# Merging two branches by pairs of column chunks, with the gates' tanh issued earlier and attention scores kept negated

## The chip, the cores and the metric

The kernel runs on one core of a Trainium2 chip. The metric is the device time of one execution in microseconds (us). Five engines work side by side, each through its own instructions in order: PE multiplies matrices, DVE does elementwise work and reductions, ACT does elementwise functions (exponential, logarithm, tanh) and casts, POOL does small extra work, SP issues transfers. An engine that must wait for another holds everything that is queued behind the waiting instruction.

## The reference

One layer of a decoder trunk over 512 tokens of 1024 channels, cut to what bears on the change:

```
h    = rmsnorm(x)
proj = h @ w_in                      # mLSTM q,k,v,o,i,f | attention q,k,v | gates ga, gb
hm   = head_rmsnorm(mlstm(...))      # 4 heads of 128, branch A
# branch B: differential attention, 4 heads, query blocks of 128
s    = q k^T / 8 + bias              # two score matrices per head, causal
a    = softmax(s1) - lam * softmax(s2)
hd   = head_rmsnorm(a @ v) * (1 - lam_init)
ya, yb = (sigmoid(o) * hm) @ w_br_m, hd @ w_br_d
x    = x + (sigmoid(ga) * ya + sigmoid(gb) * yb) @ w_out
# then the gated feed-forward layer, a per-layer embedding and a last norm
```

## The kernel before

Everything is kept channel-major: 128 channels in the partitions, the 512 tokens along the row. Every float32 product is made of three products of rounded parts (`mm3`, L94 to L98: high by high, low by high, high by low), so a product over k blocks of 128 is 3k matmuls of 128x512. Each weight chunk (128x1024) goes through `wload` (L100 to L107): SP loads `raw`, ACT casts it to `whi` (L88), DVE makes the rest `wlo` (L89). Each of the three has two buffers, so a cast waits until PE has read the chunk that is two before it.

The order of the work up to the merge is the string ORDER (projections, mLSTM heads m0 to m3, attention heads a0 to a3, their norms A and N, and eight gate projections ga0 to ga3 and gb0 to gb3). A scheduler then interleaves the instructions of each engine by priority and dependence; within an engine the order is fixed once it is built.

An attention head (`attention`, L459) takes four query blocks, each with two score matrices. For a score matrix PE makes `ds` (L468), DVE adds the bias and takes the row's greatest value (L472), negates it (L475), ACT takes the exponential with that as bias and sums the row (L476), DVE takes the reciprocal of the sum (L477). Then DVE scales and combines the two (L480, L481), PE turns the result (`at`, L487), ACT and DVE split it (`aph`, `apl`, L88 and L89), PE multiplies it with v (`av`). `attention_end` (L491) squares `av`, PE sums the squares over the channels (`hd3ss` for head 3, L168 and L169), and `rsqrt_of` (L152) makes the inverse root: Ln (L157) and Exp (L159) on ACT, Square (L160), two DVE steps (L161, L162). A product (L497) and a split give `hdh` and `hdl` (L91, L92), which PE multiplies with the branch weights.

The merge loop (L550 to L565) makes one column chunk of 128 channels at a time: both gates' tanh (L555), eight weight blocks that hold the chunk's four blocks for `ya` and its four for `yb`, 24 matmuls into two result banks of the group `mm` (four banks), then DVE and ACT combine them into `mxh`, `mxl`. Gates of the chunks 4 to 7 are projected just before their chunk, 24 matmuls each. Tanh and Ln need different function tables on ACT; a load of a table is an instruction of its own, and the gates' tanh are held by `issue_after(last_exp.ins)` behind the last Exp of a norm.

Of the kernel before, what the change touches and what calls it, by code (L numbers as in the profile page):

```python
# [11 lines left out]
F32 = mybir.dt.float32  # L12
F32R = mybir.dt.float32r
AF = mybir.ActivationFunctionType
ALU = mybir.AluOpType

P = 128
S = 512
D = 1024
KD = D // P  # L20
# [35 lines left out]
def trunk_kernel(ctx, tc, xT, pT, par, biasT, lamv, w_if, w_in, w_v, w_br, w_out, w_up,  # L56
                 w_down, w_gate, w_ple, gfin, out):
    nc = tc.nc
# [3 lines left out]
    tp = ctx.enter_context(tc.tile_pool(name="tp", bufs=1))  # L62
# [6 lines left out]
    def rt(tag, name):  # L69
        return big.tile([P, S], F32R, tag=tag, name=name, bufs=NBUF[tag])  # L70
# [5 lines left out]
    def ps(tag, name, n=S):  # L76
        return pp.tile([P, S], F32, tag=tag, name=name, bufs={"mm": 4, "sc": 2, "acc": 2}[tag])[:, :n]
# [8 lines left out]
    def split(hi, lo, src, scale=None):  # L86
        if scale is None:
            nc.scalar.copy(hi, src)  # L88
            nc.vector.tensor_sub(lo, src, f(hi))  # L89
        else:  # L90
            nc.scalar.activation(hi, src, AF.Copy, scale=scale)  # L91
            nc.vector.scalar_tensor_tensor(lo, src, scale, f(hi), op0=ALU.mult, op1=ALU.subtract)  # L92
# [7 lines left out]
    def wload(src, n=1024):  # L100
        raw = wp.tile([P, 1024], F32, tag="raw", name="raw", bufs=2)
        hi = wp.tile([P, 1024], F32R, tag="whi", name="whi", bufs=2)
        lo = wp.tile([P, 1024], F32R, tag="wlo", name="wlo", bufs=2)
        with tc.high_priority(offset=180):
            nc.sync.dma_start(raw[:, :n], src)
            split(hi[:, :n], lo[:, :n], raw[:, :n])
        return hi, lo  # L107
# [4 lines left out]
    def proj(o, w, k0, acts, start=True, stop=True):  # L112
        n = len(acts)
        for i, a in enumerate(acts):
            mm3(o, wk(w, k0 + i), a, start and i == 0, stop and i == n - 1)
# [14 lines left out]
    lnb = cp.tile([P, 1], F32, name="lnb")  # L130
# [16 lines left out]
            nc.scalar.activation(q, src, AF.Square)  # L147
            nc.vector.tensor_add(acc, acc, q)

    last_exp = None  # L150

    def rsqrt_of(r, v, a, before=None):  # L152

        if before is not None:
            with tc.issue_after(before.ins):
                nc.scalar.preload_act_table_set("natural_log_exp_and_others")
        nc.scalar.activation(r, v, AF.Ln, scale=2.0 ** -LN_SHIFT)  # L157
        nonlocal last_exp
        last_exp = nc.scalar.activation(r, r, AF.Exp, scale=-0.5, bias=lnb)  # L159
        nc.scalar.activation(a, r, AF.Square)  # L160
        nc.vector.scalar_tensor_tensor(a, v, -0.5, a, op0=ALU.mult, op1=ALU.mult)  # L161
        nc.vector.scalar_tensor_tensor(r, a, 1.5, r, op0=ALU.add, op1=ALU.mult)  # L162
# [19 lines left out]
    acc = tt("mo", "acc")  # L182
# [273 lines left out]
        return hi, lo  # L456


    def attention(hh, q, k):  # L459
        av = []  # L460
        for i in range(NB):
            n = (i + 1) * P
            nw = max(n, 2 * P)
            es, sums = [], []
            for z in range(2):
                s = ps("sc", f"ds{hh}{i}{z}", nw)
                for b in range(2):
                    nc.tensor.matmul(s, lhsT=q[z][:, i * P:(i + 1) * P], rhs=k[z][b][:, :nw],  # L468
                                     start=b == 0, stop=b == 1)
                e = tt("e" if z == 0 else "rb", f"e{z}", n)  # L470
                mx = tp.tile([P, 4], F32, tag="mx", name="mx", bufs=8)
                nc.vector.tensor_tensor_reduce(  # L472
                    out=e, in0=s[:, :n], in1=bias[hh][:, S - n:], scale=1.0, scalar=-3.0e38,
                    op0=ALU.add, op1=ALU.max, accum_out=mx[:, 0:1])
                nc.vector.tensor_scalar_mul(mx[:, 1:2], mx[:, 0:1], -1.0)  # L475
                nc.scalar.activation(e, e, AF.Exp, bias=mx[:, 1:2], accum_out=mx[:, 2:3])  # L476
                nc.vector.reciprocal(mx[:, 3:4], mx[:, 2:3])  # L477
                es.append(e)
                sums.append(mx[:, 3:4])
            nc.vector.tensor_scalar(es[1], es[1], sums[1], nlam, op0=ALU.mult, op1=ALU.mult)  # L480
            nc.vector.scalar_tensor_tensor(es[0], es[0], sums[0], es[1], op0=ALU.mult, op1=ALU.add)  # L481
            av.append(es[0])
        o = ps("acc", f"av{hh}")
        for j in range(NB):
            tps = ps("sc", f"at{hh}{j}", S - j * P)
            for i in range(j, NB):
                nc.tensor.transpose(tps[:, (i - j) * P:(i - j + 1) * P], av[i][:, j * P:(j + 1) * P], ident)  # L487
            weighted("a", j, lambda a, b: split(a, b, tps), dv, hh, (o,))
        return o
# [12 lines left out]
    def gate(c, name):  # L502
        o = ps("mm", name)
        proj(o, win(c), 0, h)
        t = tt("x", name)
        nc.vector.tensor_mul(t, o, rB)
        return t
# [3 lines left out]
    mq, mk, dq, dk, mo, sums, hm, hd, ga, gb = ({} for _ in range(10))  # L511
    for step in ORDER.split():
        what, i = step[:-1], int(step[-1])
# [18 lines left out]
        elif what == "bias":  # L532
            bias, nlam = make_bias(), make_nlam()
# [12 lines left out]
    hm, hd = ([t[i] for i in range(H)] for t in (hm, hd))  # L546


    mixed = []
    for j in range(KD):  # L550
        ta = ga[j] if j in ga else gate(20 + j, "ga")
        tb = gb[j] if j in gb else gate(28 + j, "gb")
        with tc.issue_after(last_exp.ins):
            for t in (ta, tb):
                nc.scalar.activation(t, t, AF.Tanh, scale=0.5)  # L555
        w = wload(w_br[j])
        oa, ob = ps("mm", "ya"), ps("mm", "yb")
        proj(oa, w, 0, hm)
        proj(ob, w, 4, hd)
        nc.vector.scalar_tensor_tensor(ta, ta, 1.0, oa, op0=ALU.add, op1=ALU.mult)  # L560
        nc.vector.scalar_tensor_tensor(tb, tb, 1.0, ob, op0=ALU.add, op1=ALU.mult)
        nc.vector.tensor_add(ta, ta, tb)
        hi, lo = rt("v", f"mxh{j}"), rt("v", f"mxl{j}")
        split(hi, lo, ta, 0.5)
        mixed.append((hi, lo))  # L565


    x2, h2 = [], []
    acc = tt("mo", "acc")
# [27 lines left out]
    for c in range(KF):  # L597
# [4 lines left out]
        hi, lo = rt(gtag[c], f"gh{c}"), rt(gtag[c], f"gl{c}")  # L602
# [175 lines left out]
def _chunks(w):  # L778

    k, n = w.shape  # L780
    return w.reshape(k // P, P, n // P, P).transpose(2, 1, 0, 3).reshape(n // P, P, k)
# [25 lines left out]
def _pack(x, p, rel_bias, norm_mix_g, w_in, b_if, m_conv_w, m_conv_b, m_norm_g, da_lambda, da_norm_g,  # L807
          w_br_m, w_br_d, w_out, norm_ffn_g, w_up, ffn_conv_w, ffn_conv_b, w_down, norm_ple_g,
          w_ple_gate, w_ple, norm_final_g):
    w = w_in[0]  # L810
    mq, mk, mv, mo = (w[:, 512 * i:512 * (i + 1)] for i in range(4))
    gif = np.zeros((D, 64), np.float32)
    gif[:, 0:H] = w[:, 2048:2052]
    gif[:, 32:32 + H] = w[:, 2052:2056]
    dq, dk, dv = (w[:, 2056 + 512 * i:2056 + 512 * (i + 1)] for i in range(3))
    win = np.concatenate([mq, mk, dq, dk, mo, w[:, 3592:]], axis=1)
    wv = np.concatenate([v.reshape(4, 2, P, S).transpose(0, 2, 1, 3).reshape(4, P, 2 * S) for v in (mv, dv)])
    nf = DFF // P
    order = np.stack([nf + np.arange(nf), np.arange(nf)], axis=1).ravel()
    wup = _chunks(w_up[0])[order]  # L820
    par = np.zeros((P, NPAR), np.float32)
    for c, v in ((C_GMIX, norm_mix_g[0]), (C_GFFN, norm_ffn_g[0]), (C_GPLE, norm_ple_g[0]),
                 (C_GM, m_norm_g[0]), (C_GD, da_norm_g[0])):
        v = _cols(v)
        par[:, c:c + v.shape[1]] = v
    mc = np.concatenate([m_conv_w[0], m_conv_b], axis=0)
    par[:, C_MCONV:C_MCONV + 40] = mc.reshape(5, 8, P).transpose(2, 1, 0).reshape(P, 40)
    fc = np.concatenate([ffn_conv_w[0], ffn_conv_b], axis=0)
    par[:, C_FCONV:C_FCONV + 176] = fc.reshape(4, 2 * nf, P)[:, order].transpose(2, 1, 0).reshape(P, 176)
    par[0:H, C_B] = b_if[0, :H]  # L830
    par[32:32 + H, C_B] = b_if[0, H:]
    return {
        "xT": _fmajor(x[0]), "pT": _fmajor(p[0, 0]), "par": par, "biasT": _bias_tiles(rel_bias),
        "lamv": da_lambda[0],
        "w_if": gif.reshape(KD, P, 64).transpose(1, 0, 2).reshape(P, KD * 64), "w_in": _chunks(win), "w_v": wv,
        "w_br": np.concatenate([_chunks(w_br_m[0]), _chunks(w_br_d[0])], axis=2),
        "w_out": _chunks(w_out[0]), "w_up": wup, "w_down": _chunks(w_down[0]),
        "w_gate": w_ple_gate[0].reshape(KD, P, D), "w_ple": w_ple[0].reshape(2, P, 2, S).transpose(2, 1, 0, 3).reshape(2, P, D), "gfin": norm_final_g[None],
    }
# [18 lines left out]
```

## Time and profile before

| what | value |
|---|---|
| device time, median of 3 runs | 837.1 us (836.33 to 837.5) |
| the profiled execution's own time | 836.26 us |
| its span, first to last instruction | 833.3 us |
| PE busy | 811.2 us, 97% |
| DVE busy | 539.7 us, 65% |
| ACT busy | 397.8 us, 48% |
| mean granted TensorE clock | 0.992 |

The busy shares are means over the whole span. A stage's price is read from what PE waits for in it: PE is the engine that is nearly always busy, so time is lost where it stands still or runs at a lower clock.

### The profile page before, as it was taken

To read this page: it belongs to the slowest core of one execution; us is meant where nothing else is said; L and a number is where in the kernel's file an instruction comes from. 1 tells how busy PE (TensorE), PEld (TensorE's weight loads), DVE (VectorE), ACT (ScalarE), POOL (GpSimd) and SP (SyncE) were. 2 spreads that over 40 slices of the span, in tenths; PEclk is the share of its full clock that TensorE was granted. 3 is DMA by queue.
4 is the path that set the end of the run, shared out by engine and by line. 5 is a ranking of instruction groups with operands and counts; after the bars stand their busy time and mean duration, and the time that the engine had idled before them with its cause. 6 is when DMAs were issued, how large, how long until landed. Compare 5 with 4: busy or idle time off the path is not lost.

```text
span 833.3 us, 9859 instructions
## 1 busy us (share of the span) xinstructions
PE 811.2 (97%) x3661; PEld 665.4 (80%) x3661; DVE 539.7 (65%) x873; ACT 397.8 (48%) x614; POOL 27.3 (3%) x111
## 2 busy tenths in 40 slices
PE   8999999999999699999999999999999999999995
PEld 6878878878777588888788888888888888888884
DVE  7689885589977654455677777777777333343545
ACT  6546854487664632334554444444444432232434
POOL 0011200000000000000000000000000000000000
PEclk9999999999999899999999999999999999999998
DMA  6242532212222122252322222223223323333402
GB/s 245 77 131 98 174 115 74 101 51 76 77 77 76 51 101 101 96 187 97 126 102 94 87 97 101 101 102 115 89 99 102 95 89 96 95 112 96 147 31 76
DMA packets 28119, 84.54 MB, mean 101 GB/s; under 512 B 3316, under 2 KB 4992, under 8 KB 28072
## 3 DMA queue, kind: packets, MB, share of 16 engines
q1 hardware_dynamic: 27256, 81.96, 28.9%
q0 software_dynamic: 528, 1.70, 0.7%
q8 instruction: 28, 0.46, 0.2%
q10 hardware_dynamic: 288, 0.27, 0.1%
q14 instruction: 19, 0.16, 0.1%
HBM read 81.79 MB, written 2.13 MB: 101 GB/s over the span
## 4 chain that ended last, share of the span: by engine, by line
PE 81%; ACT 2%; issue 1%; DVE 1%; POOL 0%; POOLq 0%; DVEq 0%; ACTq 0%
PE uv L96 5%; PE wd L98 5%; PE wd L96 5%; PE uv L98 5%; PE uv L97 5%; PE wd L97 5%; PE ug L96 5%; PE ug L98 5%; PE ug L97 5%; PE ga L96 2%; PE ga L98 2%; PE ga L97 2%; PE gb L98 2%; PE gb L97 2%; PE gb L96 2%; PE wo L96 2%
## 5 line engine op out<-in xcount | busy, mean ns | idle before, releaser
L88 ACT CAST whi<-raw 128x1024 fp32r<-128x1024 f32 (+1 forms) x136 | 137.7, 1013 | 221.5 <-issue 72.5
L89 DVE TENSOR_TENSOR wlo<-raw,whi 128x1024 fp32r<-128x1024 f32 (+2 forms) x135 | 159.3, 1180 | 89.5 <-ACT whi L88 88.1
L97 PE MATMUL wd<-gl,whi 128*128 128x512 f32 x176 | 68.5, 389 | 0.0
L98 PE MATMUL wd<-gh,wlo 128*128 128x512 f32 x176 | 68.5, 389 | 0.0
L96 PE MATMUL wd<-gh,whi 128*128 128x512 f32 x176 | 68.5, 389 | 0.0
L592 DVE SCALAR_TENSOR_TENSOR y<-u,prm,y 128x512 f32<-128x512 f32 x88 | 65.6, 749 | 1.5
L88 ACT CAST gh<-y 128x512 fp32r<-128x512 f32 x22 | 13.7, 622 | 55.6 <-DVE y L601 55.6
L587 DVE TENSOR_TENSOR u<-uv,rffn 128x512 f32<-128x512 f32 x22 | 15.2, 692 | 38.1 <-PE uv L98 38.1
L97 PEld LDWEIGHTS wd<-gl,whi 128*128 128x128 f32 x176 | 33.0, 188 | 6.9
L98 PEld LDWEIGHTS wd<-gh,wlo 128*128 128x128 f32 x176 | 33.0, 188 | 6.9
L96 PEld LDWEIGHTS wd<-gh,whi 128*128 128x128 f32 x176 | 33.0, 188 | 6.8
L590 ACT ACTIVATE y<-u,prm 128x512 f32<-128x512 f32 x44 | 35.7, 812 | 0.5 <-DVE u L587 0.3
L599 ACT ACTIVATE y<-y 128x512 f32<-128x512 f32 x22 | 13.9, 632 | 38.7 <-DVE y L592 38.7
L96 PE MATMUL wo<-mxh,whi 128*128 128x512 f32 x64 | 24.9, 389 | 0.0
L97 PE MATMUL wo<-mxl,whi 128*128 128x512 f32 x64 | 24.9, 389 | 0.0
L98 PE MATMUL wo<-mxh,wlo 128*128 128x512 f32 x64 | 24.9, 389 | 0.0
L89 DVE TENSOR_TENSOR gl<-y,gh 128x512 fp32r<-128x512 f32 x22 | 15.2, 692 | 14.7 <-ACT gh L88 14.7
L476 ACT ACTIVATE e<-e,mx 128x128 f32<-128x128 f32 (+3 forms) x32 | 17.8, 556 | 7.8 <-DVE mx L475 7.8
L96 PE MATMUL yb<-hdh,whi 128*128 128x512 f32 x32 | 13.2, 412 | 6.5 <-ACT hdh L91 6.5
L224 DVE SCALAR_TENSOR_TENSOR y<-u,prm,y 128x512 f32<-128x512 f32 x24 | 17.9, 744 | 0.1
L472 DVE CUSTOM_DVE_ANT_0 e<-ds,bias 128x128 f32<-128x128 f32 (+3 forms) x32 | 15.3, 484 | 3.2 <-PE ds L468 3.0
L575 DVE TENSOR_TENSOR x<-x,wo 128x512 f32<-128x512 f32 x8 | 5.5, 688 | 17.2 <-PE wo L98 17.2
(1081 smaller groups left out, 2200.8 us busy)
## 6 DMA issues: line engine op xcount, KB each, us to landing
raw<-in_w_up SPq DMA_DIRECT2D x44, 512.0 KB, 3.2
raw<-in_w_in SPq DMA_DIRECT2D x36, 512.0 KB, 3.2
raw<-in_w_down SPq DMA_DIRECT2D x16, 512.0 KB, 3.5
x<-in_xT SPq DMA_DIRECT2D x16, 256.0 KB, 4.7
raw<-in_w_br SPq DMA_DIRECT2D x8, 512.0 KB, 3.1
raw<-in_w_out SPq DMA_DIRECT2D x8, 512.0 KB, 3.3
raw<-in_w_gate SPq DMA_DIRECT2D x8, 512.0 KB, 3.3
raw<-in_w_down SPq DMA_DIRECT2D x8, 384.0 KB, 3.1
```

Of the source, the lines that this page charges most:

```text
L88: nc.scalar.copy(hi, src)
L89: nc.vector.tensor_sub(lo, src, f(hi))
L96: nc.tensor.matmul(o, lhsT=lh, rhs=rh, start=start, stop=False)
L97: nc.tensor.matmul(o, lhsT=lh, rhs=rl, start=False, stop=False)
L98: nc.tensor.matmul(o, lhsT=ll, rhs=rh, start=False, stop=stop)
L224: nc.vector.scalar_tensor_tensor(y, u[:, i:i + S], col(c0 + i), y, op0=ALU.mult, op1=ALU.add)
L472: nc.vector.tensor_tensor_reduce(out=e, in0=s[:, :n], in1=bias[hh][:, S - n:], scale=1.0, scalar=-3.0e38, op0=ALU.add, op1=ALU.max, accum_ ...
L476: nc.scalar.activation(e, e, AF.Exp, bias=mx[:, 1:2], accum_out=mx[:, 2:3])
L587: nc.vector.tensor_mul(u[:, 2:514], o, rB)
L590: nc.scalar.activation(y, u[:, 2:514], AF.Identity, scale=col(c0 + 2), bias=col(c0 + 3))
L592: nc.vector.scalar_tensor_tensor(y, u[:, i:i + S], col(c0 + i), y, op0=ALU.mult, op1=ALU.add)
L599: nc.scalar.activation(gt, gt, AF.Gelu_apprx_tanh)
```

## The change

Three edits. In `attention` the scores are kept negated: the same DVE instruction now takes scale -1 and the least value, which is at once the bias of the exponential (scale -1), so the negation (L475) goes; the two row sums of a query block lie side by side and take one reciprocal. In the merge two column chunks are made together: first the two `ya`, from one weight chunk that holds both chunks' blocks of branch A, then the two `yb` from another, and for the pair 2, 3 the two `ya` lie in result banks of the group `acc`. The early gates' tanh are held behind the last softmax exponential instead of the last Exp of a norm. The host packs the branch weights to suit.

```diff
-        last_exp = nc.scalar.activation(r, r, AF.Exp, scale=-0.5, bias=lnb)
+        nc.scalar.activation(r, r, AF.Exp, scale=-0.5, bias=lnb)
...
-                    out=e, in0=s[:, :n], in1=bias[hh][:, S - n:], scale=1.0, scalar=-3.0e38,
-                    op0=ALU.add, op1=ALU.max, accum_out=mx[:, 0:1])
-                nc.vector.tensor_scalar_mul(mx[:, 1:2], mx[:, 0:1], -1.0)
-                nc.scalar.activation(e, e, AF.Exp, bias=mx[:, 1:2], accum_out=mx[:, 2:3])
-                nc.vector.reciprocal(mx[:, 3:4], mx[:, 2:3])
+                    out=e, in0=s[:, :n], in1=bias[hh][:, S - n:], scale=-1.0, scalar=3.0e38,
+                    op0=ALU.add, op1=ALU.min, accum_out=mx[:, z:z + 1])
+                last_softmax = nc.scalar.activation(e, e, AF.Exp, scale=-1.0, bias=mx[:, z:z + 1],
+                                                    accum_out=mx[:, 2 + z:3 + z])
                 es.append(e)
-                sums.append(mx[:, 3:4])
-            nc.vector.tensor_scalar(es[1], es[1], sums[1], nlam, op0=ALU.mult, op1=ALU.mult)
-            nc.vector.scalar_tensor_tensor(es[0], es[0], sums[0], es[1], op0=ALU.mult, op1=ALU.add)
+            nc.vector.reciprocal(mx[:, 4:6], mx[:, 2:4])
+            nc.vector.tensor_scalar(es[1], es[1], mx[:, 5:6], nlam, op0=ALU.mult, op1=ALU.mult)
+            nc.vector.scalar_tensor_tensor(es[0], es[0], mx[:, 4:5], es[1], op0=ALU.mult, op1=ALU.add)
...
-    for j in range(KD):
-        ta = ga[j] if j in ga else gate(20 + j, "ga")
-        tb = gb[j] if j in gb else gate(28 + j, "gb")
-        with tc.issue_after(last_exp.ins):
-            for t in (ta, tb):
+    for m in range(0, KD, 2):
+        js = (m, m + 1)
+        gates = [(ga[j] if j in ga else gate(20 + j, "ga"), gb[j] if j in gb else gate(28 + j, "gb")) for j in js]
+        with tc.issue_after(last_softmax.ins):
+            for t in (t for pr in gates for t in pr):
                 nc.scalar.activation(t, t, AF.Tanh, scale=0.5)
-        w = wload(w_br[j])
-        oa, ob = ps("mm", "ya"), ps("mm", "yb")
-        proj(oa, w, 0, hm)
-        proj(ob, w, 4, hd)
...
+        outs = []
+        for n, (tag, ys) in enumerate((("acc" if m == 2 else "mm", hm), ("mm", hd))):
+            w = wload(w_br[m + n])
+            outs.append([ps(tag, ("ya", "yb")[n]) for _ in js])
+            for i in range(2):
+                proj(outs[n][i], w, 4 * i, ys)
```

How it moves instructions, at three places.

PE around the sum of squares of the last attention head, before (`hd3ss` is that sum, `hdh3` the finished head 3, `yb` the branch B product):

```order
L169 MATMUL hd3ss_2680<-cspl_2682,ones_89 128x512
L97 MATMUL yb_2748<-hdl0_1771,whi_2742 128x512
L98 MATMUL yb_2748<-hdh0_1770,wlo_2743 128x512
L96 MATMUL yb_2748<-hdh1_1930,whi_2742 128x512
L97 MATMUL yb_2748<-hdl1_1931,whi_2742 128x512
L98 MATMUL yb_2748<-hdh1_1930,wlo_2743 128x512
L96 MATMUL yb_2748<-hdh2_2258,whi_2742 128x512
L97 MATMUL yb_2748<-hdl2_2259,whi_2742 128x512
L98 MATMUL yb_2748<-hdh2_2258,wlo_2743 128x512
L96 MATMUL yb_2707<-hdh3_2694,whi_2701 128x512
```

The same place in the changed kernel (`whi_2639`, `whi_2671` and `whi_2721` are the first three branch chunks):

```order
L166 MATMUL hd3ss_2616<-cspl_2618,ones_89 128x512
L96 MATMUL ya_2645<-hmh3_2366,whi_2639 128x512
L97 MATMUL ya_2645<-hml3_2367,whi_2639 128x512
L98 MATMUL ya_2645<-hmh3_2366,wlo_2640 128x512
...
L98 MATMUL yb_2677<-hdh2_2210,wlo_2672 128x512
L96 MATMUL ya_2726<-hmh0_1875,whi_2721 128x512
...
L96 MATMUL ya_2727<-hmh0_1875,whi_2721 128x512
L97 MATMUL ya_2727<-hml0_1876,whi_2721 128x512
L96 MATMUL yb_2676<-hdh3_2630,whi_2671 128x512
L96 MATMUL yb_2677<-hdh3_2630,whi_2671 128x512
```

Before, 8 matmuls stand between the end of the sum and the first use of head 3; now 35 do (3 of the second `ya`, 9 and 9 of the first two `yb`, 12 of the third `ya`, 2 of the fourth).

ACT from the cast of head 3's squares (`csph`) to the finished head 3, before:

```order
L166 CAST csph_2681<-v_2676 128x512
L157 ACTIVATE r_2677<-v_2676 128x512
L159 ACTIVATE r_2677<-r_2677,lnb_91 128x512
L555 ACT_TABLE_LOAD
L555 ACTIVATE ga_2293<-ga_2293 128x512
L160 ACTIVATE hd3ss_2680<-r_2677 128x512
L555 ACTIVATE gb_2640<-gb_2640 128x512
L555 ACTIVATE ga_2673<-ga_2673 128x512
L555 ACTIVATE gb_2359<-gb_2359 128x512
L555 ACTIVATE ga_2326<-ga_2326 128x512
L555 ACTIVATE gb_2607<-gb_2607 128x512
L555 ACTIVATE ga_2061<-ga_2061 128x512
```

The same in the changed kernel, from the last tanh on:

```order
L556 ACTIVATE ga_2609<-ga_2609 128x512
L163 CAST csph_2617<-v_2612 128x512
L88 CAST whi_2721<-raw_2720 128x1024
L155 ACT_TABLE_LOAD
L155 ACTIVATE r_2613<-v_2612 128x512
L156 ACT_TABLE_LOAD
L156 ACTIVATE r_2613<-r_2613,lnb_91 128x512
L157 ACTIVATE hd3ss_2616<-r_2613 128x512
L91 ACTIVATE hdh3_2630<-y_2611 128x512
L88 CAST whi_2753<-raw_2752 128x1024
```

The eight tanh and their table load have left the stretch between Exp and `hdh3`; a weight cast and two table loads have come into it.

ACT ahead of that, in the changed kernel, between the last softmax exponential (`e1`) and the split of head 3's turned scores (`aph`):

```order
L476 ACTIVATE e1_2428,mx_2418<-e1_2428,mx_2418 128x512
L88 CAST whi_2639<-raw_2638 128x1024
L556 ACT_TABLE_LOAD
L556 ACTIVATE ga_2245<-ga_2245 128x512
L556 ACTIVATE gb_2576<-gb_2576 128x512
L556 ACTIVATE gb_2311<-gb_2311 128x512
L556 ACTIVATE ga_2278<-ga_2278 128x512
L88 CAST aph_2440<-at30_2435 128x512
```

Before, only the weight cast stood there; the load and four tanh are new.

## Rows read from the trace of the kernel before

**Rows 1.** The page: busy time, share of the span and instructions of PE.

```profile
PE 811.2 (97%) x3661; PEld 665.4 (80%) x3661; DVE 539.7 (65%) x873; ACT 397.8 (48%) x614; POOL 27.3 (3%) x111
```

**Rows 2.** What PE waited for: us in total, times, longest.

```profile
PE yb L96 <- ACT hdh L91: 6.5, 1, 6.5
...
PE s L96 <- ACT mk0h L91: 1.4, 1, 1.4
```

**Rows 3.** Chain that ended last, around that wait: start, us, what.

```profile
272.41 0.70 DVE v L495
...
273.14 0.64 ACT r L157
...
273.80 0.72 ACT r L159
...
274.54 1.28 ACT L555
...
275.84 0.63 ACT ga L555
276.46 0.49 ACT hd3ss L160
...
277.50 0.52 ACT ga L555
...
280.01 0.62 ACT hdh L91
```

**Rows 4.** Timeline of PE: start, us, instruction, and idle time before it.

```profile
271.95 0.42 PE L169 MATMUL hd3ss<-cspl,ones 128*128 128x512 f32 x1
...
273.81 0.39 PE L98 MATMUL yb<-hdh,wlo 128*128 128x512 f32 x1
280.68 0.79 PE L96 MATMUL yb<-hdh,whi 128*128 128x512 f32 x1 [6.48 <-ACT hdh L91]
...
284.84 0.40 PE L98 MATMUL ya<-hmh,wlo 128*128 128x512 f32 x1
...
289.19 0.39 PE L97 MATMUL yb<-hdl,whi 128*128 128x512 f32 x1
...
295.08 0.39 PE L96 MATMUL ga<-h0h,whi 128*128 128x512 f32 x1
```

**Rows 5.** Windows: length, busy PE, PEld, DVE, ACT, POOL, granted clock, DMA share, GB/s.

```profile
59.00:62.00 3.00, 1.58 (x8) 0.91 (x6) 2.30 (x3) 2.62 (x5) 2.02 (x3) 1.00 0.36 119
...
277.00:278.00 1.00, 0.00 (x0) 0.00 (x0) 0.97 (x3) 1.00 (x3) 0.00 (x0) 0.92 0.00 0
...
281.00:284.00 3.00, 3.00 (x7) 2.08 (x7) 1.69 (x3) 1.67 (x3) 0.00 (x0) 0.50 0.00 0
...
300.00:310.00 10.00, 10.00 (x46) 8.29 (x45) 4.53 (x5) 3.16 (x4) 0.00 (x0) 1.00 0.24 82
```

**Rows 6.** Timeline of DVE and ACT, head 3's chain and a weight cast.

```profile
277.10 0.69 DVE L161 SCALAR_TENSOR_TENSOR hd3ss<-v,hd3ss 128x512 f32<-128x512 f32 x1
277.83 0.69 DVE L162 SCALAR_TENSOR_TENSOR r<-hd3ss,r 128x512 f32<-128x512 f32 x1
...
279.03 0.68 DVE L497 TENSOR_TENSOR y<-y,r 128x512 f32<-128x512 f32 x1
...
289.66 1.05 ACT L88 CAST whi<-raw 128x1024 fp32r<-128x1024 f32 x1 [0.32 <-PE yb L97]
```

**Rows 7.** DVE's groups from 155 to 285 us: line, count, busy us, mean ns, idle.

```profile
L477 DVE RECIPROCAL mx<-mx 128x1 f32<-128x1 f32 x32 | 4.2, 156 | 0.1
L475 DVE TENSOR_SCALAR mx<-mx 128x1 f32<-128x1 f32 x32 | 4.2, 145 | 0.3
```

**Rows 8.** What PE's weight loads waited for, the attention's own lines.

```profile
PEld av L96 <- ACT aph L88: 2.3, 6, 0.6
PEld ds L468 <- DVE mx L472: 1.8, 8, 0.3
```

**Rows 9.** Timeline where head 3's turned scores are split.

```profile
264.41 0.97 ACT L88 CAST aph<-at 128x512 fp32r<-128x512 f32 x2 [2.72 <-PE at L487]
```

More of the change, by code (lines that the diff above doesn't have):

```diff
@@ L148, in sumsq_add @@
             nc.vector.tensor_add(acc, acc, q)
-    last_exp = None
     def rsqrt_of(r, v, a, before=None):
@@ L157, in rsqrt_of @@
         nc.scalar.activation(r, v, AF.Ln, scale=2.0 ** -LN_SHIFT)
-        nonlocal last_exp
-        last_exp = nc.scalar.activation(r, r, AF.Exp, scale=-0.5, bias=lnb)
+        nc.scalar.activation(r, r, AF.Exp, scale=-0.5, bias=lnb)
         nc.scalar.activation(a, r, AF.Square)
@@ L456, in mlstm_norm @@
         return hi, lo
+    last_softmax = None
     def attention(hh, q, k):
+        nonlocal last_softmax
         av = []
@@ L463, in attention @@
             nw = max(n, 2 * P)
-            es, sums = [], []
+            es = []
+            mx = tp.tile([P, 6], F32, tag="mx", name="mx", bufs=8)
             for z in range(2):
@@ L470, in attention @@
                 e = tt("e" if z == 0 else "rb", f"e{z}", n)
-                mx = tp.tile([P, 4], F32, tag="mx", name="mx", bufs=8)
                 nc.vector.tensor_tensor_reduce(
-                    out=e, in0=s[:, :n], in1=bias[hh][:, S - n:], scale=1.0, scalar=-3.0e38,
-                    op0=ALU.add, op1=ALU.max, accum_out=mx[:, 0:1])
-                nc.vector.tensor_scalar_mul(mx[:, 1:2], mx[:, 0:1], -1.0)
-                nc.scalar.activation(e, e, AF.Exp, bias=mx[:, 1:2], accum_out=mx[:, 2:3])
-                nc.vector.reciprocal(mx[:, 3:4], mx[:, 2:3])
+                    out=e, in0=s[:, :n], in1=bias[hh][:, S - n:], scale=-1.0, scalar=3.0e38,
+                    op0=ALU.add, op1=ALU.min, accum_out=mx[:, z:z + 1])
+                last_softmax = nc.scalar.activation(e, e, AF.Exp, scale=-1.0, bias=mx[:, z:z + 1],
+                                                    accum_out=mx[:, 2 + z:3 + z])
                 es.append(e)
-                sums.append(mx[:, 3:4])
-            nc.vector.tensor_scalar(es[1], es[1], sums[1], nlam, op0=ALU.mult, op1=ALU.mult)
-            nc.vector.scalar_tensor_tensor(es[0], es[0], sums[0], es[1], op0=ALU.mult, op1=ALU.add)
+            nc.vector.reciprocal(mx[:, 4:6], mx[:, 2:4])
+            nc.vector.tensor_scalar(es[1], es[1], mx[:, 5:6], nlam, op0=ALU.mult, op1=ALU.mult)
+            nc.vector.scalar_tensor_tensor(es[0], es[0], mx[:, 4:5], es[1], op0=ALU.mult, op1=ALU.add)
             av.append(es[0])
@@ L549, in trunk_kernel @@
     mixed = []
-    for j in range(KD):
-        ta = ga[j] if j in ga else gate(20 + j, "ga")
-        tb = gb[j] if j in gb else gate(28 + j, "gb")
-        with tc.issue_after(last_exp.ins):
-            for t in (ta, tb):
-                nc.scalar.activation(t, t, AF.Tanh, scale=0.5)
-        w = wload(w_br[j])
-        oa, ob = ps("mm", "ya"), ps("mm", "yb")
-        proj(oa, w, 0, hm)
-        proj(ob, w, 4, hd)
[L560 to L565, printed above, removed]
+    for m in range(0, KD, 2):
[3 more added lines that the diff above has]
+            for t in (t for pr in gates for t in pr):
+                nc.scalar.activation(t, t, AF.Tanh, scale=0.5)
+        outs = []
[4 more added lines that the diff above has]
+                proj(outs[n][i], w, 4 * i, ys)
+        for i, j in enumerate(js):
+            ta, tb = gates[i]
+            nc.vector.scalar_tensor_tensor(ta, ta, 1.0, outs[0][i], op0=ALU.add, op1=ALU.mult)
+            nc.vector.scalar_tensor_tensor(tb, tb, 1.0, outs[1][i], op0=ALU.add, op1=ALU.mult)
+            nc.vector.tensor_add(ta, ta, tb)
+            hi, lo = rt("v", f"mxh{j}"), rt("v", f"mxl{j}")
+            split(hi, lo, ta, 0.5)
+            mixed.append((hi, lo))
     x2, h2 = [], []
@@ L835, in _pack @@
         "w_if": gif.reshape(KD, P, 64).transpose(1, 0, 2).reshape(P, KD * 64), "w_in": _chunks(win), "w_v": wv,
-        "w_br": np.concatenate([_chunks(w_br_m[0]), _chunks(w_br_d[0])], axis=2),
+        "w_br": np.stack([_chunks(v[0]).reshape(4, 2, P, S).transpose(0, 2, 1, 3).reshape(4, P, 2 * S)
+                          for v in (w_br_m, w_br_d)], axis=1).reshape(KD, P, 2 * S),
         "w_out": _chunks(w_out[0]), "w_up": wup, "w_down": _chunks(w_down[0]),
```

## The prediction, written before the changed kernel ran

> **What bounds the kernel now.** I read the page first: PE is busy for 811.2 of 833.3 us [rows 1], so time can only be won where PE stands still or runs slowly, and an engine beside it costs nothing until PE waits for it. The second view, PE's waits over the whole span, tells where that is: one wait of 6.5 us; the others are far smaller, as the 1.4 us for `mk0h` [rows 2]. PE waits there for ACT, for the finished attention head 3 (`hdh3`). Third, the chain that ended last, around it: PE's sum of squares ends, DVE makes `v` at 272.41, ACT does Ln, Exp, then a table load and a tanh ahead of the Square, and more tanh between the Square and `hdh3`, which starts at 280.01 [rows 3]. Fourth, PE's timeline: the sum's second matmul starts at 271.95, the last matmul that needs nothing of head 3 at 273.81, the next one at 280.68 [rows 4]. At full rate a matmul follows the one before it after 0.227 us (26 steps from 289.19 to 295.08 [rows 4]), so PE was free at 274.04 and stood for 6.64. Fifth, the windows: the granted clock stays at 1.00 (2.4 GHz) through a stop of 1.4 us at 60 us, but here it reads 0.92 at 277 to 278 and 0.50 (1.2 GHz) at 281 to 284 [rows 2, 5]. From 280.68 to 284.84 PE makes nine steps [rows 4]; at 0.227 they take 2.04, so the low clock, and in it a short wait for `hdl3`, cost 2.12. The place loses 6.64 + 2.12 = 8.76 us, and no other place of this kernel comes near.
>
> **The merge by pairs: cover for PE.** As the order of PE shows, 8 matmuls stand between the sum and the first use of head 3 before, 35 after. Their number in the whole kernel is the same, so this moves 27 x 0.227 = 6.12 us of work from behind the stop to ahead of it. Counted from the start of the sum's second matmul, PE had work for 274.04 - 271.95 = 2.09; it now has 8.21. That holds if the chunks are there: the third one, `whi_2721`, is wanted 23 matmuls after the sum, at some 5.3, and is cast by 2.0 (next part), its rest `wlo` one DVE step later.
>
> **The tanh moved: the chain to `hdh3`.** Before, the chain took 8.73 (271.95 to 280.68). Of it go the load and the tanh ahead of the Square, the merge's product between two of DVE's steps, and ACT's wait in the tanh queue. What comes in are a weight cast and two table loads, since the tanh now leave the tanh table behind and Ln and Exp each get a load. The weight cast waits until PE has read the first branch chunk for the last time, two matmuls after the sum, at 0.50; from such a matmul's start to the cast it took 289.66 - 289.19 = 0.47 [rows 4, 6]. So, step by step from the sum's start: cast 0.97 to 2.02 [rows 6]; load to 3.32, 1.30 with its gap; Ln to 3.98, 0.66; load to 5.28; Exp to 6.02, 0.74; Square to 6.65, taken like the 0.62 of the cast `hdh` and a gap (its own piece in the chain is 0.49) [rows 3]. Then DVE: 277.10 to 277.83 is 0.73 for a step that needs the one before it [rows 6], twice, 8.11; the product `y` 0.68 and a gap, 8.83; `hdh3` to PE 280.68 - 280.01 = 0.67 [rows 3, 4], 9.50. PE thus still stops, for 9.50 - 8.21 = 1.3 us: the chain is 0.8 longer than before, the cover 6.1 longer. `hdl3` is no wait any more, since three other matmuls stand ahead of its first use. A stop of 1.3 is as short as the one at 60 us, where the clock stayed at 1.00 [rows 2, 5], so I count no low clock behind it.
>
> **The tanh ahead of the split.** A load and four tanh now stand ahead of head 3's `aph` on ACT: 1.28 + 4 x 0.52 = 3.4 us [rows 3]. ACT had 2.72 us of idle time there [rows 9]. The difference, 0.6, delays `aph` and what follows it, up to the sum, if PE reaches it as early as before; two more tanh and a weight cast stand ahead of the second pair of splits. Bounds: 0, if DVE brings the scores later anyway, and 3.4, if that idle time is gone. I take 0.4, near the row, and 0.1 for the `wlo` of the fourth chunk, which can only be begun after `hdh3`.
>
> **The attention edit: nothing by itself.** It takes 32 negations of 0.145 and 16 of 32 reciprocals of 0.156 off DVE, 4.6 + 2.5 = 7.1 us [rows 7], some 1.8 a head. PE hides them now: all that it waits for in the attention is 2.3 us for `aph` in six places and 1.8 for score results in eight [rows 8], much of it a tenth of a us when PE changes tiles. So the edit can give 4.1 at most. The other bound is above zero: the scheduler has used the shorter chains to bring the turns of the scores forward. In head 3 the PE work between the last score product and the first turn that needs it falls, by the order of both kernels, from 36 to 27 matmuls, 2.0 us, against the 1.8 that DVE saves; in head 0 from 27 to 24, in the other two by one more or less. I take 0 and keep -1 to +2. The reduction with scale -1 and least is the same instruction at the same shape: between 0 and one negation's 0.145 each, on DVE. A reciprocal of two values costs between one and two rows of 0.156, and the exponential's scale nothing that ACT's row would show.
>
> A rule speaks against the moved tanh. The two new loads cost me 1.28 each, because ACT's first tanh starts 0.02 after the load's end, 275.84 against 274.54 + 1.28 [rows 3]. The Trainium skill, page ScalarE: Activation LUTs, section What ACT_TABLE_LOAD costs, gives 1283 ns for the load and about 1380 ns more for a drain at every change of table; the section Table sets: the hidden batching unit wants all work of one table done before the next, which the new order breaks twice in the chain. By the page's figures, an estimate, the chain would be 2 x 1.38 = 2.8 longer and the stop 4.1 in place of 1.3. No drain shows in this trace, so the row decides.
>
> **The sum.** 8.76 - 1.3 - 0.4 - 0.1 = 7.0 us less. The profiled execution's own time is 836.26, of which 833.3 are the span and 3.0 lie around it and stay: 829.3. The median of the runs is 0.8 higher, 837.1, from which the same sum gives 830.1. I take 829.7.
>
> **Rivals.**
> *New waits in the attention.* PE's order there is tighter, as worked out, and DVE was almost never idle in it. If DVE's chains don't keep up in heads 0 and 3, PE stops for up to 0.7 and 2.0 more, and a late `aph` adds up to 1: 832 to 833.5. For it: `av` and `ds` are waited for already [rows 8]. Against: DVE's saving of 1.8 a head is of the same size.
> *The stop stays long.* If ACT needs as long again around each load as the load's row, 2 x 1.28, the stop is 3.9, and then the clock falls too: before it read 0.92 some 3 us into the stop [rows 5]. 3.9 + 2.1 in place of 1.3 gives 834.4. A late transfer ahead of the cast would do the same. Against it: the 0.02 behind the load [rows 3], and a transfer that has been free to start since the first chunk was split, several us earlier. The skill's drain, above, would bring just this case.
> *Slower: result banks.* A pair holds four result banks of `mm`, all there are, where one chunk held two. The next gate must wait until DVE has taken the first `ya`. If DVE came to that late, PE would stop ahead of the pairs 4, 5 and 6, 7 and ahead of the output projection. It decides from the point where DVE is later than the 24 matmuls, 5.4 us, that PE does for `yb` in the meantime; to end slower than before, the three stops must eat 7.0, or 2.3 each, 838 and more. Against it: DVE is busy for 4.53 of 10 us in this stage [rows 5].
> *The change doesn't do what it says.* If head 3's chain were late for another reason, say its squares come 6 us later since the tanh sit ahead, the cover would be used up and the time stay at 836 to 837.
>
> **How the numbers follow.** The forecast, 827.2 to 832 around 829.7, gets 0.74; its lower end is a stop that vanishes (1.3) and 1 won in the attention. New waits in the attention 0.13, the long stop 0.05, a gain beyond 827.2 0.02, nothing 0.03, slower 0.03. The range 827.2 to 832.8 leaves out just under 2 in 10, most of it above. A change of 0.2%, 1.7 us, is about what a measurement of this kernel can tell from none. Every case but the last two is faster by more: faster 0.94, within 0.2% 0.03, slower 0.03.
>
> **What would show it.** PE's longest wait, still `yb` for `hdh`, falls from 6.5 to between 0.8 and 1.8, and no window of the merge reads a clock of 0.50. In the chain, ACT shows two table loads around Ln, with no gap behind them, and a weight cast ahead of them. From the sum to `hdh3`'s first matmul 9.5 us pass, 8.2 of them filled. PE's waits for `aph` stay within a us in all of what they were, and the pairs 4 to 7 run without a stop. I am wrong if the sum of squares itself comes more than 1 us later than 272, if the long wait keeps over 3 us, or if a stop appears ahead of a gate projection.

## The result, and the profile after

The changed kernel takes 829.65 us, the median of 4 runs (828.52 to 831.11), against 836.72 us (835.06 to 837.5, 4 runs) for the kernel before beside it: a ratio of 0.9919, 95% interval 0.9896 to 0.9943. Measured once more on another occasion it took 829.28, ratio 0.9921 (0.9908 to 0.9934). The profiled execution took 828.52 us, of which 826.4 are the span (before 836.26 and 833.3). Two single executions further down, 901.5 us with the tanh late and 1014.31 us with four copies, were slow throughout (mean granted clock 0.85 and 0.75) and are left out of the medians and ratios.

The page, its busy times and its row of granted clocks (in tenths, 40 slices):

```profile
PE 810.0 (98%) x3661; PEld 664.4 (80%) x3661; DVE 536.1 (65%) x825; ACT 400.8 (49%) x616; POOL 27.3 (3%) x111
...
PEclk9999999999999999999999999999999999999998
```

PE does the same 3661 matmuls in 1.2 us less busy time [rows 1]; the span falls by 6.9. So most of what went, 5.7 us, is idle time of PE, not its work. The row of clocks had an 8 in its 14th place before (271 to 292 us), and has none there now. DVE lost 48 instructions and 3.6 us of busy time; the single instructions add up to 7.1, as foreseen, but the records of neighbours overlap (DVE's come to 572.2 us in all for 536.1 busy). ACT's two more are table loads.

What PE waited for: total us, times, longest.

```profile
...
PE s L96 <- ACT mk0h L91: 1.4, 1, 1.4
...
PE yb L96 <- ACT hdh L91: 1.1, 1, 1.1
```

The wait of 6.5 us [rows 2] is still the same wait, of the same instruction for the same tile, but it is 1.1 long. PE's timeline there (start, us, instruction, idle before it) shows how far the cover goes:

```profile
269.38 0.42 PE L166 MATMUL hd3ss<-cspl,ones 128*128 128x512 f32 x1
...
277.37 0.39 PE L97 MATMUL ya<-hml,whi 128*128 128x512 f32 x1
278.86 0.73 PE L96 MATMUL yb<-hdh,whi 128*128 128x512 f32 x2 [1.10 <-ACT hdh L91]
279.43 0.40 PE L98 MATMUL ya<-hmh,wlo 128*128 128x512 f32 x1
```

From the sum's second matmul to the end of the last independent one PE has work for 277.37 + 0.23 - 269.38 = 8.22 us; before it was 2.09 [rows 4]. The first matmul on head 3 starts 9.48 us after the sum's second. PE stands for the difference, 1.26. The chain that ended last (start, us, what) shows what fills the 9.48:

```profile
270.30 1.05 ACT whi L88
271.35 0.02 issue
271.37 1.28 ACT L155
272.65 0.01 issue
272.66 0.63 ACT r L155
273.30 0.02 issue
273.31 1.28 ACT L156
274.60 0.01 issue
274.61 0.73 ACT r L156
275.34 0.02 issue
275.37 0.61 ACT hd3ss L157
275.98 0.02 issue
276.00 0.71 DVE hd3ss L158
276.71 0.02 issue
276.73 0.70 DVE r L159
277.43 0.02 issue
277.45 0.70 DVE y L497
278.16 0.02 issue
278.18 0.64 ACT hdh L91
```

The tanh of [rows 3] are gone; a weight cast and two table loads stand in their place, and after each load the next instruction starts 0.01 later. The Trainium skill, page ScalarE: Activation LUTs, section What ACT_TABLE_LOAD costs, adds about 1380 ns of drain to a load; no drain shows behind either.

The windows of the changed kernel, which answer to the 0.92 and 0.50 of [rows 5] (length, busy PE, PEld, DVE, ACT, POOL, granted clock, DMA share, GB/s):

```profile
278.00:279.00 1.00, 0.14 (x1) 0.14 (x2) 0.91 (x3) 0.63 (x1) 0.00 (x0) 1.00 0.00 0
279.00:282.00 3.00, 3.00 (x14) 2.46 (x15) 1.75 (x3) 0.99 (x1) 0.00 (x0) 1.00 0.00 0
```

PE makes 14 matmuls in the three microseconds behind the stop, where it made 7 before at half the clock. In the attention, the waits of [rows 8] hardly moved:

```profile
PEld ds L469 <- DVE mx L473: 1.9, 8, 0.3
PEld av L96 <- ACT aph L88: 1.9, 6, 0.4
```

### The profile page after: what moved, and what is told of

It is laid out like the page before. It is cut to its first block, busy times and chain, and to the rows that moved or that the text cites. A ratio compares the mean times of both kernels' runs of the same rounds, so it can differ in the third digit from the quotient of the medians.

```text
span 826.4 us, 9812 instructions
## 1 busy us (share of the span) xinstructions
PE 810.0 (98%) x3661; PEld 664.4 (80%) x3661; DVE 536.1 (65%) x825; ACT 400.8 (49%) x616; POOL 27.3 (3%) x111
## 4 chain that ended last, share of the span: by engine, by line
PE 81%; ACT 2%; issue 1%; DVE 1%; POOL 0%; POOLq 0%; DVEq 0%; ACTq 0%
PE wd L97 5%; PE wd L96 5%; PE uv L98 5%; PE uv L97 5%; PE uv L96 5%; PE wd L98 5%; PE ug L98 5%; PE ug L97 5%; PE ug L96 5%; PE ga L97 2%; PE gb L96 2%; PE ga L96 2%; PE gb L97 2%; PE ga L98 2%; PE gb L98 2%; PE wo L96 2%
## 5 line engine op out<-in xcount | busy, mean ns | idle before, releaser
L591 POOL MEMSET u<- 128x2 f32 x44 | 4.3, 99 | 361.5 <-DVE y L597 351.6
```

## The experiments

Two accounts stood against each other. The first, *cover against chain*: PE stops for the time that head 3 takes from the sum's second matmul to its first use (the chain), less the work that the order of PE puts in between (the cover: 0.27 for that second matmul and 0.227 for each that follows); where the matmuls come from doesn't matter. The second keeps the prediction's bookkeeping: the pairs give the cover, the attention edit gives nothing, the tanh shorten the chain. All of one group ran on the same chip beside the kernel before; the single edits are one group, the changed kernel's second measurement with the one load, the late and the last tanh another, and the rest a third, on another chip. Across groups only the ratios compare.

### One edit of the three at a time

Attention edit alone (the rest of the diff undone):

```diff
...
-                nc.vector.tensor_scalar_mul(mx[:, 1:2], mx[:, 0:1], -1.0)
-                nc.scalar.activation(e, e, AF.Exp, bias=mx[:, 1:2], accum_out=mx[:, 2:3])
-                nc.vector.reciprocal(mx[:, 3:4], mx[:, 2:3])
...
+                last_softmax = nc.scalar.activation(e, e, AF.Exp, scale=-1.0, bias=mx[:, z:z + 1],
+                                                    accum_out=mx[:, 2 + z:3 + z])
...
+            nc.vector.reciprocal(mx[:, 4:6], mx[:, 2:4])
```

> The attention edit alone; merge by single chunks, tanh behind the last Exp of a norm, both as before. Theory 1, cover against chain, whatever edit gives the cover: the order of PE shows 29 matmuls between the sum of squares of head 3 and the first use of head 3 (8 before, 35 in the changed kernel), so PE has work for 0.27 + 29 x 0.227 = 6.9 us from the start of the sum's second matmul. The chain stays that of before, 8.7. PE stops for some 1.9 in place of 6.6 and the clock does not fall; a weight cast that waits for yb of the first chunk may add 0.7 to 2. The merge then loses 2.6 to 4 in place of 8.8: 831 to 833, say 832. Theory 2, the prediction's own wording, in which the pairs give the cover and the attention edit gives nothing by itself: 836.7, within 1 us. A stop of 6 us or more for hdh would refute theory 1.

832.24 us, ratio 0.9944 (0.9929 to 0.9959). The first account holds. PE's timeline of this kernel:

```profile
274.12 0.39 PE L98 MATMUL yb<-hdh,wlo 128*128 128x512 f32 x1
276.22 0.73 PE L96 MATMUL yb<-hdh,whi 128*128 128x512 f32 x2 [1.71 <-ACT hdh L91]
...
278.58 0.79 PE L96 MATMUL ya<-hmh,whi 128*128 128x512 f32 x1 [0.38 <-ACT whi L88]
```

276.22 - 274.12 - 0.23 = 1.87 of stop, as 8.73 - 6.86 gives, and 0.6 more for a weight cast. One thing was missed: the clock did fall behind the first stop, as this kernel's window shows:

```profile
278.00:281.00 3.00, 2.62 (x7) 1.94 (x7) 3.00 (x4) 1.48 (x2) 0.00 (x0) 0.50 0.00 0
```

Pairs alone:

```diff
-    for j in range(KD):
+    for m in range(0, KD, 2):
...
         with tc.issue_after(last_exp.ins):
```

> The merge by pairs alone; scores and the place of the tanh as before. Theory 1, cover against chain: 34 matmuls stand between the sum and the first use of head 3, cover 0.27 + 34 x 0.227 = 8.0 us; the chain to hdh3 keeps a table load and tanh and gets the cast of the fourth branch chunk ahead of hdh3, some 9.1. PE stops once for 1.1, early (for that cast, which waits for the end of the second ya) or late (for hdh3), and the clock does not fall: a loss of 1.2 to 1.5 in place of 8.8, so 829.5, 7 us less than before. Theory 2, that the early tanh are needed to shorten the chain: with them late the chain is longer by a load and the tanh ahead of hdh3, 1.3 + 4 x 0.52 = 3.4, the stop 4 or more and the low clock is back: 833 to 835.

828.49 us, ratio 0.9905 (0.9891 to 0.992). The pairs alone give all that the three edits give. PE stops once, for 1.32, and for the cast of the fourth branch chunk; when it comes to head 3, at 283.57, ACT has ended `hdh` (282.60 + 0.63 = 283.23). PE's timeline:

```profile
281.20 0.39 PE L98 MATMUL ya<-hmh,wlo 128*128 128x512 f32 x1
282.75 0.50 PE L96 MATMUL yb<-hdh,whi 128*128 128x512 f32 x1 [1.16 <-ACT whi L88]
```

Early tanh alone:

```diff
-        with tc.issue_after(last_exp.ins):
+        with tc.issue_after(last_softmax.ins):
```

> The early tanh alone; merge by single chunks and scores as before. Theory 1, cover against chain: only 6 matmuls stand between the sum and the first use of head 3, cover 1.6 us. The chain loses the tanh and their load and gets two loads around Ln, and has no weight cast in it: 7.3. Stop 5.7, and behind it the low clock for some 2: 7.7 lost in place of 8.8, so 835.7, 1 us less than before. Theory 2, that the tanh are what frees the chain and do most of the work: a stop under 3 us and 831 or less. Theory 3, that the early tanh hold up head 3's scores: 837 and more, with a PE wait for aph of a us or more.

836.12 us, ratio 0.9996 (0.9987 to 1.0005): no change that can be told. The chain is 7.38 in place of 8.73, but two matmuls of cover are gone too, and the wait stays:

```profile
PE yb L96 <- ACT hdh L91: 5.6, 1, 5.6
```

The clock falls behind it as before, but while PE works it is low for longer: 5.5 us from 281.79 on, where it was 4.0 from 280.68 on. PE's steps there lose 2.8 us in place of 2.1, which takes back 0.7 of the 0.9 us less of stop, and the times show no gain.

Pairs and tanh, attention edit undone (the diff of the change without its part in `attention`):

```diff
         with tc.issue_after(last_softmax.ins):
...
+                nc.vector.tensor_scalar_mul(mx[:, 1:2], mx[:, 0:1], -1.0)
```

> The merge by pairs and the early tanh; only the attention edit is undone. Theory 1, cover against chain: 32 matmuls between the sum and the first use of head 3, cover 7.5 us; a chain of 7.5 to 8.5, and a wait of about 1.1 for the cast of a branch chunk; loss 1 to 1.5, so 829.5: the attention edit is worth nothing once the pairs are there. Rival, that the shorter DVE chains of the attention edit bear part of the gain in heads 0 to 3: 831 or more, with waits for ds, av or aph that are 1.5 us longer in sum than in the changed kernel.

828.38 us, ratio 0.9905 (0.9888 to 0.9922). PE's one stop is 1.07, for the cast, as expected. The changed kernel's ratio is 0.992 in both of its groups, with intervals that overlap this one, so no gain by the attention edit shows once the pairs are there.

### Where the cover comes from

By the order of PE, counted between the start of the merge and head 3's first use:

| kernel | merge matmuls ahead of the sum | behind it (cover) | cover, us | chain, us | stop by account, us | measured, us |
|---|---|---|---|---|---|---|
| before | 34 | 8 | 2.09 | 8.73 | 6.6 | 6.64 |
| attention alone | 13 | 29 | 6.86 | 8.73 | 1.9 | 1.87 |
| pairs alone | 35 | 34 | 8.0 | 9.2 | 1.2 | 1.32, for the cast |
| tanh alone | 36 | 6 | 1.63 | 7.38 | 5.7 | 5.74 |
| changed kernel | 21 | 35 | 8.22 | 9.48 | 1.3 | 1.26 |
| one load (below) | 21 | 28 | 6.63 | 6.80 | 0.2 | 0.18 |
| tanh late (below) | 13 | 44 | 10.26 | 10.2 | 0 | 0.0 |
| tanh last (below) | 13 | 30 | 7.08 | 7.12 | 0.0 | 0.05 |

Chain and stop are from PE's timeline of each kernel's profiled execution: the chain from the second sum matmul to head 3's first, the stop the step into that matmul less 0.227. With the pairs alone and the tanh late PE doesn't wait for head 3; there the chain ends with ACT's `hdh`, and 0.05 on top, as in the kernels where PE waits for it. Where PE waits for head 3, chain less cover is the stop by construction, and the row proves nothing; what tests the account is that the expectations named the stops ahead of the runs. With single chunks 42 merge matmuls need nothing of head 3 (12 `ya` and 9 `yb` in each of two chunks), and 34 of them were spent before the sum. The pairs make the stock larger: the pairs alone have 69. The attention edit leaves it at 42, but the scheduler brings the sum forward past 21 of them, which then lie behind it. Two ways fill the same hole, so their gains don't add: 4 and 8 us apart, 7 together.

That the gain lies here and not elsewhere shows by stage. What PE loses from the sum to the last branch matmul (each step from start to start less 0.227 us for 512 columns) is 8.7 us before, 4.2 with the attention edit alone, 1.4 with the pairs alone, 8.5 with the tanh alone, 1.1 with pairs and tanh, and 1.5 in the changed kernel, in both of its profiles. Behind that matmul it is 2.6 in every kernel, and between attention head 0's first score and the sum it moves by 1 us at most (6.3 to 7.3).

### The chain of the changed kernel

> The changed kernel once more, on the same chip as the three beside it, so that differences of one us can be told: 829.7 again, within 0.8.

829.28 us: as told above.

One load ahead of Ln for Ln and Exp:

```diff
-        rsqrt_of(r, v, ss, None if hh else last)
+        rsqrt_of(r, v, ss, last if hh in (0, H - 1) else None)
```

> The changed kernel, but with one table load ahead of head 3's Ln that serves Ln and Exp, issued behind the cast of the squares, in place of a load each. Theory 1, cover against chain: the load now ends ahead of the weight cast (csph ends 0.8 before the sum's second matmul, the load takes 1.28), so the chain loses both loads, 2.6 us: hdh3 reaches PE at 6.9 in place of 9.5. The order has 28 matmuls of cover in place of 35, 6.6 us. Stop 0.3 in place of 1.3: 828.7, 1 us less than the changed kernel beside it. Rival 1, the two loads had cost more than their rows show: the stop is gone altogether and hdh3 comes over 3.5 earlier. Rival 2, the stop isn't set by the loads but by the cast of the third branch chunk ahead of them: no change, 829.7, with a wait for hdh or whi of a us or more.

828.3 us, ratio 0.991 (0.9895 to 0.9924). The chain is 6.80 (from 269.84), 2.7 less, which is twice the load's 1.28 and the gaps, and nothing more. PE hardly stops:

```profile
276.23 0.39 PE L96 MATMUL ya<-hmh,whi 128*128 128x512 f32 x1
276.64 0.73 PE L96 MATMUL yb<-hdh,whi 128*128 128x512 f32 x2
```

The gain of 1 us by the medians is of the stop's size. The intervals overlap, so the times alone don't prove it.

Tanh held behind the last Exp again, the rest of the change kept:

```diff
-        with tc.issue_after(last_softmax.ins):
+        with tc.issue_after(last_exp.ins):
```

> The changed kernel, but with the early tanh held behind the last Exp of a norm, as before. Theory 1, cover against chain: the order puts 44 matmuls between the sum and the first use of head 3, cover 10.3 us; the chain has a load, eight tanh and a weight cast ahead of hdh3, 10.5. Stop 0.2 to 0.5, and no tanh ahead of aph: 828.3, 1.4 less than the changed kernel beside it, so the early tanh cost a little. Rival, the early tanh are a needed part of the gain: with them late PE stops for 3 us or more and the clock falls to 0.50 behind it: 832 to 834.

828.32 us, ratio 0.9907 (0.9893 to 0.9921). The chain is long, 10.2 from 269.49 on, and wholly covered: ACT ends `hdh` at 279.02 + 0.62 = 279.64, before PE is free, as PE's timeline shows (279.52 is the last independent matmul):

```profile
279.52 0.39 PE L98 MATMUL ya<-hmh,wlo 128*128 128x512 f32 x1
279.75 0.68 PE L96 MATMUL yb<-hdh,whi 128*128 128x512 f32 x2
```

The gain doesn't need the early tanh.

Tanh held behind the finished head 3:

```diff
-            nc.scalar.activation(hi, src, AF.Copy, scale=scale)
+            c = nc.scalar.activation(hi, src, AF.Copy, scale=scale)
...
-        split(hi, lo, y, 1.0 - LAM_INIT)
+        last_head = split(hi, lo, y, 1.0 - LAM_INIT)
...
-        with tc.issue_after(last_softmax.ins):
+        with tc.issue_after(last_head.ins):
```

> The changed kernel, but with the early tanh held behind the finished head 3 (its cast hdh3), so that Ln, Exp and Square run in their own table with no load and no tanh between. Theory 1, cover against chain: chain Ln 1.2, Exp 1.9, Square 2.6, two DVE steps and the product, hdh3 at PE by 6.1 us after the start of the sum's second matmul; 30 matmuls of cover, 7.1. No stop at all, and no tanh ahead of aph: 828.0, 1.7 less than the changed kernel beside it and the fastest of all. Rival, the late tanh hold up the result banks instead: DVE can free the banks of the first pair only behind its tanh, PE then stops ahead of the second pair's yb or of the gates 4 and 5: 829.5 or more, with a new PE wait of 1.5 us or more there.

827.37 us, ratio 0.9895 (0.9882 to 0.9909), the lowest median of all: 1.9 us under the changed kernel in the same group (827.37 to 829.28), with no execution of the one as long as any of the other. From attention head 0's first score to the last branch matmul PE loses some 1.0 us less than in the changed kernel, 7.4 for 8.4 and 8.5 in its two profiles; where the other 0.9 lies isn't shown. The one-load kernel loses 7.2 there, and its interval overlaps, so which of the two is faster stays open. ACT's timeline shows Ln, Exp and Square with no load between them, and the tanh behind `hdh`:

```profile
269.47 0.63 ACT L156 ACTIVATE r<-v 128x512 f32<-128x512 f32 x1 [2.04 <-DVE v L499]
270.13 0.72 ACT L157 ACTIVATE r<-r,lnb 128x512 f32<-128x512 f32 x1
270.89 0.60 ACT L158 ACTIVATE hd3ss<-r 128x512 f32<-128x512 f32 x1
271.43 1.04 ACT L88 CAST whi<-raw 128x1024 fp32r<-128x1024 f32 x1
274.72 0.63 ACT L91 ACTIVATE hdh<-y 128x512 fp32r<-128x512 f32 x1 [2.25 <-DVE y L501]
275.37 1.28 ACT L560 ACT_TABLE_LOAD   x1
276.66 0.63 ACT L560 ACTIVATE ga<-ga 128x512 f32<-128x512 f32 x1
```

The chain was 7.12 (from 268.28), not 6.1: DVE made a weight chunk's `wlo` ahead of `y`. The cover of 7.08 just reaches it:

```profile
275.12 0.39 PE L97 MATMUL ya<-hmh,whi 128*128 128x512 f32 x1
275.40 0.74 PE L97 MATMUL yb<-hdh,whi 128*128 128x512 f32 x2
```

The same place for the tanh, with the attention edit undone:

```diff
-        with tc.issue_after(last_exp.ins):
+        with tc.issue_after(last_head.ins):
```

> The fastest so far (early tanh behind the finished head 3), with the attention edit undone. Theory 1: 26 matmuls of cover, 6.2 us, for a chain of 6.1, so no stop for hdh3; but the cast of the fourth branch chunk waits until PE has read the third for the last time, which is just ahead of its use, and PE stops for 1.1 to 1.3 there, as with the pairs alone: 828.4, 1 us more than with the attention edit. Rival, the attention edit is dead weight here: 827.4 or less, no wait for whi over 0.5.

828.58 us, ratio 0.9913 (0.9899 to 0.9928), near the 828.4 expected. PE had no stop for `hdh`, and lost 0.7 for the fourth chunk's `wlo` and 0.23 ahead of its `whi`, 0.9 in all for the 1.1 to 1.3 foreseen, and most of it for `wlo`, which was not. That the attention edit is worth 1 us in this company stays open: the intervals overlap.

### Banks, and a longer chain

Third pair of `ya` in `mm`:

```diff
-        for n, (tag, ys) in enumerate((("acc" if m == 2 else "mm", hm), ("mm", hd))):
+        for n, (tag, ys) in enumerate((("mm", hm), ("mm", hd))):
```

> The changed kernel, but the third pair of ya lies in banks of mm, as the other pairs, instead of acc. The order of PE is the same. Theory 1: the first ya have been taken by DVE long before, since their tanh are early, so the banks don't matter: 829.5, within 0.8 of the changed kernel. Rival, the prediction's one on result banks: PE must wait for DVE to free the first ya, a stop of over 1 us ahead of the third ya: 830.5 or more, and the low clock if it adds to the stop for hdh3.

830.16 us, ratio 0.9929 (0.9915 to 0.9942): the same as the changed kernel within the intervals. PE's list of waits has the same wait at the merge and no new one there:

```profile
PE yb L96 <- ACT hdh L91: 1.1, 1, 1.1
```

Extra copies in head 3's chain (`extra` is 4, then 8, for head 3 and 0 elsewhere):

```diff
         nc.scalar.activation(r, v, AF.Ln, scale=2.0 ** -LN_SHIFT)
+        for _ in range(extra):
+            nc.scalar.copy(r, r)
```

> The changed kernel with four extra in-place copies of r on ACT between head 3's Ln and Exp (they change no value): the chain to hdh3 is 4 x 0.6 = 2.4 us longer, 11.9 in place of 9.5. Theory 1, cover against chain: the scheduler knows of them and its order has 48 matmuls of cover in place of 35, 0.27 + 48 x 0.227 = 11.2 us; stop 0.7, and no low clock: 829.0, no slower than the changed kernel although 2.4 us of work were put into the chain that ends last. Rival, the chain itself decides: the stop is 1.3 + 2.4 = 3.7, the clock falls behind it, 2 more: 834.

829.42 us, ratio 0.9925 (0.9911 to 0.994): 3.1 us more chain (12.57), and the ratio is that of the changed kernel; the rival's 834 is out. The stop was not the one expected, though, 0.7 for `hdh`: PE's steps show 1.07 for a weight cast and 0.23 for `hdh` behind it. In PE's list:

```profile
PE yb L96 <- ACT whi L88: 0.9, 1, 0.9
```

> The same with eight copies, 4.8 us more chain than in the changed kernel. Theory 1: 58 matmuls of cover, but the last 13 need the fourth branch chunk, whose cast now stands behind Square on ACT: PE reaches it at 0.27 + 45 x 0.227 = 10.5 us after the start of the sum's second matmul, the cast ends at 12.1; then hdh3 comes at 14.0, inside the cover. So the wait is for whi, not for hdh, 1.7 us, and up to 1.2 for its wlo behind DVE's steps of the chain. Whether the clock falls behind a stop of that length: it stayed at 1.00 behind 1.57 (60 us) and fell behind 1.87 (attention edit alone), so it is open. 830 to 831.5 without, up to 833.5 with it. Rival, the chain decides: 1.3 + 4.8 = 6.1 of stop and the low clock: 836.5.

832.17 us, ratio 0.9953 (0.9937 to 0.997). The wait is for `whi`, as expected, but by PE's steps it is 2.33 in place of 1.7. Most of that comes from the chain ahead of the cast: a copy takes 0.65, not 0.6, eight times. Its wait in the list and two windows:

```profile
PE yb L96 <- ACT whi L88: 2.2, 1, 2.2
```

```profile
281.00:284.00 3.00, 1.24 (x5) 0.72 (x5) 2.52 (x4) 1.42 (x2) 0.00 (x0) 1.00 0.00 0
284.00:287.00 3.00, 3.00 (x13) 2.46 (x14) 1.89 (x3) 0.63 (x1) 0.00 (x0) 1.00 0.48 175
```

The clock stays at 1.00. The profiled execution took 830.01, the least of six; why the median is 2 us above it isn't shown by a trace. The rival's 836.5 is out.

## Why the prediction was right, point by point

**The place and the loss.** Right: the span fell by 6.9, and the 6.64 and the low clock at this place went, down to 1.26.

**The cover.** 8.21 foreseen, 8.22 measured. Its cause was named too narrowly, under the heading of the merge by pairs: the count compared the whole change with the kernel before, and so gave the pairs what the attention edit also moves. Apart, the pairs reach 34 matmuls and the attention edit 29. A count in the order of the whole change can't be split over its edits; it takes an order of each.

**The chain.** 9.50 foreseen, 9.48 measured, with the steps as listed: cast, two loads of 1.28 without a drain, two DVE steps, product, cast. The remaining stop is 1.26 for 1.3.

**The tanh ahead of the split.** The price of 0.4 did not come: PE's wait for `aph` went from 2.3 [rows 8] to 1.9. With the tanh late it reads 2.6 in the tanh-last kernel. The losses in the attention, given in the next part, are 0.2 to 0.5 smaller with the early tanh. What they cost is elsewhere: two loads in the chain, and 8 merge matmuls that the order spends ahead of the sum (21 against 13). "The tanh moved" was costed right as a chain, 0.8 longer, but that the change would do as well without it was not considered.

**The attention edit: nothing by itself.** This step failed as worded. Alone it gives 4 us, by bringing head 3's sum forward in PE's order. Beside the pairs no gain of it shows, and only in that sense did the 0 fit. In the attention itself, from its head 0's first score to head 3's sum, PE loses 0.3 to 0.6 us more with it: 6.7 to 6.8 without and 7.3 with it where the tanh are late, 6.3 and 6.5 without and 6.8 to 6.9 with it where they are early. What in the new order costs that isn't shown. The prediction looked for its worth in the attention's own waits (4.1 at most) and not in what a shorter chain lets the scheduler put behind the sum.

**The sum.** 7.0 foreseen; the medians differ by 7.07, the spans by 6.9. That 0.4 for `aph` was wrong hardly matters, and that is luck: PE's steps beyond full rate, summed over the timeline from head 0's first score to head 3's sum (each step from start to start less 0.227 us for 512 columns, in proportion for fewer, at least 0.06), are 6.65 us before, 6.8 after and 6.9 in the second profile. So 0.2 to 0.3 did go there, but as the sum of two terms that the prediction had at 0 and at 0.4: the attention edit's loss of about 0.5 and the early tanh's gain of about 0.3.

**The rivals.** No new wait in the attention above 0.5, and no more than 0.3 us more lost there, as above; no long stop; the banks don't matter while the tanh are early (the run with `mm`) and with the tanh last no stop shows at the gates, though the third pair is in `acc` there.

**The clock.** "As short as the one at 60 us, so no low clock" came true for 1.26, but the length of the stop was a weak reason, as the last section shows.

## What to carry to other kernels

Where one engine waits for a chain on others, count two things: the chain from the timeline, and the work that the bound engine's order puts between producer and first use. Worked out ahead of the run, their difference (or the wait for a weight cast inside it) came within some 0.2 us of the stop in eight kernels here; with the extra copies and with the old scores behind the last tanh it was up to 0.6 off, and in two of these three the wait was for another tile than the one named. Several edits that fill the same hole don't add up, so undo them one at a time, and drop the one without which the time stays.

## What was not expected

Of the clock: it stayed at 1.00 behind stops of 1.26 and 1.32, and in the eight-copy kernel behind 2.33 and, 1.0 us after, 0.46. In the attention-alone kernel it fell to 0.50 at 277.9, 1.7 us after the end of a stop of 1.87 and just ahead of the next, of 0.6. The length of the stop alone doesn't tell. What does stays open.

Executions differ before any edit acts. In all fourteen profiles PE, ACT and DVE have the same order up to 162 us. Yet PE's matmul into mLSTM head 0's first score starts at 61.02 in the attention-alone profile and at 63.54 in the pairs-and-tanh profile, with the same work ahead and the same wait:

```profile
61.02 0.50 PE L96 MATMUL s<-mq0h,mk0h 128*128 128x512 f32 x1 [1.42 <-ACT mk0h L91]
```

```profile
63.54 0.50 PE L96 MATMUL s<-mq0h,mk0h 128*128 128x512 f32 x1 [1.42 <-ACT mk0h L91]
```

So 2.5 us of a difference between two single profiles can lie in the first 61 us (3.2 up to the attention's first score, near 160), as large as the differences told apart here. A profile was therefore read by stage, and kernels compared by medians of several runs.
